# Token-major projections 512 columns wide, weights loaded unit by unit, and TensorE transposes in the first segment of a hybrid mLSTM and DeltaNet layer

## The chip, the cores and the metric

The kernel runs on one core of a Trainium2 chip. Its engines are TensorE (PE: matmuls, and PEld for its weight loads), VectorE (DVE), ScalarE (ACT), GpSimd (POOL) and SyncE (SP, which issues nearly all transfers). The metric is the device time of one execution in microseconds (us), as the median of three runs.

## What is computed

One decoder layer over 2048 tokens of width 1024 in float32. Both kinds of heads read the same normalised input; four mLSTM heads and eight gated DeltaNet (GDN) heads are worked off in chunks, gated, and projected back:

```python
h = rms_norm(x, attn_norm[l])
proj = jnp.einsum('bsd,dp->bsp', h, w_in[l])
(mq, mk, mv, mo, mz, mi, mf, gqkv, gz, gb, ga) = jnp.split(proj, split_points, axis=-1)
h_m = mlstm_chunkwise(q_m, k_m, v_m, i_pre, f_pre)
y_m = h_m * jax.nn.sigmoid(mo) * jax.nn.silu(mz)          # h_m normalised before
qkv = jax.nn.silu(causal_depthwise_conv(gqkv, g_conv[l]))
o_g = gated_delta_chunkwise(q_g, k_g, v_g, log_alpha, beta)
y_g = merge_heads(o_g) * jax.nn.silu(gz)                  # o_g normalised before
x = x + jnp.einsum('bsm,md->bsd', jnp.concatenate([y_m, y_g], -1), w_out[l])
return rms_norm(x, final_norm)
```

## The kernel before

The tokens are cut into four segments of 512. In a segment the work goes pair by pair (n = 0 to 3: two GDN heads and one mLSTM head), each pair in two windows. Window P projects the pair's GDN columns: gk, gq and gv feature-major (`proj_fm`: the weights stand still and 512 tokens move, two tiles `pf_...` of 24 matmuls for each), then gz token-major (`proj_tm`: 128 tokens stand still and 256 weight columns move, four tiles `pt_gz` of 24 matmuls). For n = 0 gz comes first. Window M projects mq and mk feature-major, and then mv, mo and mz token-major, 256 columns each, 96 matmuls each. Every product is three matmuls, since weights and input are split into a high and a low part (`hi`, `lo`; `hh`, `hl`). The last segment has its windows in another order. The output projection (`po`) follows after the last segment.

A projection's tile lies in one of three PSUM buffers (`psj`); another five (`psc`) serve everything else. A tile's buffer is free for the third tile after it when its readers are done: ACT's copy into `xin` for the GDN tiles, whose depthwise convolution (three taps, L675) and silu (L681) DVE does; for mv ACT's copy (L512) and DVE's low part `vlo` (L515; not for n = 3); for gz ACT's tanh and DVE's product `gg` (L703); for mz ACT's tanh (L525) and DVE's L526. In the first segment (`raw`) the input isn't normalised yet, and tiles are scaled as they are read: `ps * rbc0` in place by DVE for feature-major, ACT with `rs0` (L365) for token-major.

k and v of the GDN are needed token-major as well. Where the tables `KTR` and `VT` (rows: first segment, middle segments, last; columns: n) hold 1, DVE does it with 32-row stream transposes (`ktok`, `gv`, L488); where they hold 0, PE transposes 128x128 blocks (`ktp`, `vp`).

Between the projections' steps `window` puts other work into PE's order, each as a stream spread over a fraction of the window (`WIN` = 41.6 cost units): `g_prep` (ktok, the products `kk`, q's norm, and the forward substitution `tb`/`xb` that inverts 32-row blocks on DVE, L825 and L829) at the start of M; `g_level` (`dmz`, `zp`, `fp`, `zq`, `fq`) and the first `CH_N` = 6 of 14 steps of `g_chain` (`sp`, `R`, `vq`, `su`, `op`, `SS`) in the next P, the other steps in the next M; `m_chunks` of the mLSTM head (`nd`, `up`, `CN`, with k transposed by DVE into `kw`, and `ptt` made from a row `nm` that SP fetches) in the next P. At the end of the segment the next segment's input is loaded and squared (`rms_stats`).

PE's order is what the code writes (`tc.manual_schedule`). The other engines are ordered when the kernel is built, by a list scheduler with priorities, and that order is fixed: an engine whose next instruction isn't ready waits.

Weights come from DRAM in units of 512 KB, with a ring of ten of them (`wu`). In the first segment each group is loaded raw, split into high and low parts, and the parts are stored for the later segments; later `load_w` fetches a group's four units one group ahead, when `next_w` is called.

Of the kernel before, what the change touches and what calls it, by code (L numbers as in the profile page):

```python
# [65 lines left out]
def hybrid_layer(  # L66
# [80 lines left out]

    def unit(ncol, dt, nm):
        return wp.tile([P, HK, ncol], dt, tag="wu", name=nm, bufs=10)

    def load_w(key, src, ncol, nm, between=None):

        if key in parts_d:
            his, los = ([unit(ncol, F32R, f"{p_}_{nm}_{i}") for i in range(2)] for p_ in ("whi", "wlo"))
            for i in range(2):
                for part, t_ in enumerate((his[i], los[i])):
                    nc.sync.dma_start(t_.bitcast(F32), parts_d[key][part, i])
            return his, los
        return split_w(key, src, ncol, nm, between)
# [1221 lines left out]
```

## Time and profile before

| | |
|---|---|
| median of three runs | 2320.91 us (2320.58 to 2321.42) |
| profiled execution | 2320.7 us |
| its span in the trace | 2318.9 us |
| busy share of the span: PE, DVE, ACT, POOL | 95%, 81%, 38%, 35% |
| first segment | 7 to 513.3 us |
| second, third, fourth segment | 513.3 to 987.2, to 1459.8, to 1938 us |
| rest of the output projection | 1938 to 2318.9 us |

Times in the trace are counted from the span's start. A window of the second segment is named by n: P(2) runs from 756.5 to 813.8, M(2) from 813.8 to 869.6. PE is the engine that is busy nearly always; the matmul records overlap, so one that lasts 0.28 us in the records can follow the last after 0.12.

### The profile page before, as it was taken

To read this page: it belongs to the slowest core of one execution; us is meant where nothing else is said; L and a number is where in the kernel's file an instruction comes from. 1 tells how busy PE (TensorE), PEld (TensorE's weight loads), DVE (VectorE), ACT (ScalarE), POOL (GpSimd) and SP (SyncE) were. 2 spreads that over 40 slices of the span, in tenths; PEclk is the share of its full clock that TensorE was granted. 3 is DMA by queue.
4 is the path that set the end of the run, shared out by engine and by line. 5 is a ranking of instruction groups with operands and counts; after the bars stand their busy time and mean duration, and the time that the engine had idled before them with its cause. 6 is when DMAs were issued, how large, how long until landed. Compare 5 with 4: busy or idle time off the path is not lost.

```text
span 2318.9 us, 41978 instructions
## 1 busy us (share of the span) xinstructions
PE 2212.4 (95%) x14750; PEld 1964.7 (85%) x14750; DVE 1888.6 (81%) x5359; ACT 875.5 (38%) x2351; POOL 800.4 (35%) x1220
## 2 busy tenths in 40 slices
PE   8889999998999999998999999999999999999998
PEld 7778888887989898888898989888988997788887
DVE  7989898997988888879888888798757737887784
ACT  5545555544342424343334243443344234111111
POOL 4646565561211111423021214221212114555543
PEclk9999999999999999999999999999999999999999
DMA  7766667674445454654455546454546454222321
GB/s 268 248 222 225 227 216 256 212 257 159 159 160 182 160 191 159 231 182 155 154 185 175 188 166 236 146 180 172 188 163 210 160 195 151 84 94 94 102 84 64
DMA packets 183323, 409.20 MB, mean 176 GB/s; under 512 B 51736, under 2 KB 84632, under 8 KB 183112
## 3 DMA queue, kind: packets, MB, share of 16 engines
q1 hardware_dynamic: 182392, 405.74, 51.4%
q8 instruction: 116, 1.90, 0.3%
q14 instruction: 95, 0.78, 0.1%
q10 hardware_dynamic: 720, 0.79, 0.1%
HBM read 309.68 MB, written 96.90 MB: 175 GB/s over the span
## 4 chain that ended last, share of the span: by engine, by line
PE 56%; DVE 30%; DMA 7%; ACT 3%; issue 2%; POOL 1%; SPq 1%; ACTq 0%; POOLq 0%; DVEq 0%
PE po L1237 5%; PE po L1236 5%; PE po L1235 5%; DVE ktok L488 3%; DVE xb L829 3%; DVE tb L825 3%; DVE kw L488 2%; DVE gv L488 2%; PE pt_mo L359 2%; PE pt_mo L360 2%; PE pt_mo L361 2%; PE pt_gz L361 2%; PE pt_mz L359 2%; PE pt_gz L360 2%; PE pt_gz L359 2%
## 5 line engine op out<-in xcount | busy, mean ns | idle before, releaser
L1196 DVE STREAM_TRANSPOSE ytt<-yl 32x256 f32<-32x256 f32 x448 | 195.3, 436 | 45.4 <-POOL ylo L1164 39.4
L993 POOL TENSOR_TENSOR gms<-gms,nhalf 128x2 f32<-128x2 f32 x64 | 47.2, 738 | 413.6 <-DVE gms L991 408.5
L825 DVE TENSOR_TENSOR tb<-xb,lbt 128x248 f32<-128x248 f32 (+30 forms) x496 | 168.0, 339 | 21.0 <-DMA lbt<-l_d 8.0
L829 DVE TENSOR_TENSOR xb<-xb,tb 128x248 f32<-128x248 f32 (+30 forms) x496 | 168.7, 340 | 12.7
L359 PE MATMUL pt_mv<-whi_M,hh 128*128 128x256 f32 x512 | 150.5, 294 | 14.4 <-DVE vlo L515 10.5
L359 PE MATMUL pt_gz<-whi_P,hh 128*128 128x256 f32 (+1 forms) x512 | 153.1, 299 | 1.4 <-ACT whi_P L175 1.1
L359 PE MATMUL pt_mz<-whi_M,hh 128*128 128x256 f32 x512 | 149.5, 292 | 4.0 <-DVE tz L526 3.4
L359 PE MATMUL pt_mo<-whi_M,hh 128*128 128x256 f32 x512 | 149.0, 291 | 1.7 <-DVE vlo L515 1.7
L361 PE MATMUL pt_gz<-whi_P,hl 128*128 128x256 f32 (+1 forms) x512 | 148.5, 290 | 1.9 <-DVE hl L336 1.9
L360 PE MATMUL pt_gz<-wlo_P,hh 128*128 128x256 f32 (+1 forms) x512 | 148.5, 290 | 0.8 <-DVE wlo_P L178 0.8
L361 PE MATMUL pt_mv<-whi_M,hl 128*128 128x256 f32 x512 | 146.9, 287 | 0.0
L360 PE MATMUL pt_mv<-wlo_M,hh 128*128 128x256 f32 x512 | 146.8, 287 | 0.0
L360 PE MATMUL pt_mz<-wlo_M,hh 128*128 128x256 f32 x512 | 145.2, 284 | 0.0
L361 PE MATMUL pt_mz<-whi_M,hl 128*128 128x256 f32 x512 | 145.2, 284 | 0.0
L361 PE MATMUL pt_mo<-whi_M,hl 128*128 128x256 f32 x512 | 144.5, 282 | 0.0
L360 PE MATMUL pt_mo<-wlo_M,hh 128*128 128x256 f32 x512 | 144.5, 282 | 0.0
L1244 ACT ACTIVATE jkf<-xr 128x512 f32<-128x512 f32 (+1 forms) x33 | 20.4, 619 | 266.9 <-DVE xr L1242 143.5
L488 DVE STREAM_TRANSPOSE ktok<-gk 32x128 f32<-32x128 f32 x384 | 116.2, 303 | 5.4
L488 DVE STREAM_TRANSPOSE gv<-xingv 32x128 f32<-32x128 f32 x384 | 116.1, 302 | 5.4
L1235 PE MATMUL po<-woh,yh 128*128 128x512 f32 (+1 forms) x297 | 114.6, 386 | 1.1 <-ACT yh L1162 1.1
L1236 PE MATMUL po<-wol,yh 128*128 128x512 f32 (+1 forms) x297 | 114.7, 386 | 0.9 <-POOL wol L1042 0.9
L1237 PE MATMUL po<-woh,ylo 128*128 128x512 f32 (+1 forms) x297 | 114.8, 387 | 0.1
(403 smaller groups left out, 7581.0 us busy)
## 6 DMA issues: line engine op xcount, KB each, us to landing
whi_M<-wdM SPq DMA_DIRECT2D x96, 512.0 KB, 3.9
wlo_M<-wdM SPq DMA_DIRECT2D x96, 512.0 KB, 5.6
whi_P<-wdP SPq DMA_DIRECT2D x90, 512.0 KB, 4.0
wlo_P<-wdP SPq DMA_DIRECT2D x90, 512.0 KB, 5.1
wraw_M<-in_wg_dram SPq DMA_DIRECT2D x32, 512.0 KB, 6.7
wdM<-whi_M SPq DMA_DIRECT2D x32, 512.0 KB, 3.7
wdM<-wlo_M SPq DMA_DIRECT2D x32, 512.0 KB, 5.3
wraw_P<-in_wg_dram SPq DMA_DIRECT2D x30, 512.0 KB, 6.3
```

The lines of the kernel that those rows point to most:

```text
L359: nc.tensor.matmul(ps, lhsT=hh[k][:, ts], rhs=hi, start=(k == 0), stop=False)
L360: nc.tensor.matmul(ps, lhsT=hh[k][:, ts], rhs=lo, start=False, stop=False)
L361: nc.tensor.matmul(ps, lhsT=hl[k][:, ts], rhs=hi, start=False, stop=(k == KT - 1))
L488: nc.vector.transpose(dst[32 * a:32 * a + 32, :, 32 * b:32 * b + 32], s4[32 * b:32 * b + 32, :, a, :])
L825: nc.vector.tensor_tensor(tb[:, :, 0:n], xb[:, :, i:i + 1].broadcast_to([P, 8, n]), lbt[:, i:i + 1, i + 1:32].broadcast_to([P, 8, n]), op= ...
L829: nc.vector.tensor_tensor(xs, xs, tb[:, :, 0:n], op=ALU.subtract)
L993: nc.gpsimd.tensor_tensor(ms, ms, nhalf[:, 0:2], op=ALU.pow)
L1196: nc.vector.transpose(ytt[32 * b:32 * b + 32, :, 32 * a:32 * a + 32], y3[32 * a:32 * a + 32, :, 32 * b:32 * b + 32])
L1235: nc.tensor.matmul(ps, lhsT=yh, rhs=woh, start=(k == 0), stop=False)
L1236: nc.tensor.matmul(ps, lhsT=yh, rhs=wol, start=False, stop=False)
L1237: nc.tensor.matmul(ps, lhsT=ylo, rhs=woh, start=False, stop=(k == 15))
L1244: nc.scalar.activation(jk[:, 0:n], xr[:, cs], AF.Square, accum_out=ssf[:, i:i + 1])
```

## The change

- From the second segment on, mo and mz of a head are one projection 512 columns wide (`proj_tm_wide`): two tiles at a time, step by step in turn, in two passes over the weights. gz of pair n and mv of head n are likewise one (`wide_z`: n = 1 to 3 of the second and third segment, n = 1 of the fourth), and it stands at the start of M, ahead of mq and mk. Its tiles are called `pt_mv`; gz is the left half, mv the right.
- Window P then ends with gv. The cost units by which streams are spread are 31 for such P windows and 52 for such M windows, and the chain gets 4 of its steps in P instead of 6 (`CH_NW`; n = 1 to 3 of the middle segments).
- The stored parts of two groups that go together lie side by side, and units are loaded whenever the ring has one free (`freed`, `pump`).
- In the first segment k and v are transposed by PE in all pairs, DVE writes the scaled feature-major tiles straight to their place (`fm_out`), and mv and mo are scaled by the instruction that reads them.

```diff
+NU = 10
...
+CH_NW = 4
...
-VT = ((0, 1, 1, 1), (1, 1, 1, 1), (1, 0, 0, 0))
-KTR = ((0, 1, 1, 1), (1, 1, 1, 1), (0, 1, 0, 0))
+VT = ((0, 0, 0, 0), (1, 1, 1, 1), (1, 0, 0, 0))
+KTR = ((0, 0, 0, 0), (1, 1, 1, 1), (0, 1, 0, 0))
...
+    ring = {"free": NU}
+    coming = []
...
+        if isinstance(key, list):
+            w = Weights(nm, 512, 2)
+            kept = parts_d[key[0]][0]
+            w.due = [((p_, i), kept[p_, i // 2, :, i % 2 * 2:i % 2 * 2 + 2]) for i in range(4) for p_ in range(2)]
...
+    def pump():
+        while coming and ring["free"] > 0:
+            w = coming[0]
+            at, src = w.due.pop(0)
+            t_ = w.units[at] = unit_(w.rows, w.n, F32R, f"w{at[0]}_{w.nm}_{at[1]}")
+            nc.sync.dma_start(t_.bitcast(F32), src)
+            ring["free"] -= 1
+            if not w.due:
+                wready.append(coming.pop(0))
+
+    def freed(n):
+        ring["free"] += n
+        if not wloads:
+            pump()
...
-        kept = parts_d[key] = ypool.tile([2, 2, P, HK, ncol], F32, tag=f"wd{nm}", name=f"wd{nm}")
+        pair = next((p_ for p_ in WIDE if key in p_), None)
+        c0 = pair.index(key) * ncol if pair else 0
+        if c0:
+            kept = parts_d[pair[0]][0]
+        else:
+            kept = ypool.tile([2, 2, P, HK, 512 if pair else ncol], F32, tag=f"wd{nm}", name=f"wd{nm}")
+        parts_d[key] = kept, c0, ncol
...
+    WIDE = [[("M", n, 2), ("M", n, 3)] for n in range(4)] + [[("P", n, 3), ("M", n, 1)] for n in range(1, 4)]
+
+    def wide_z(seg, n):
+
+        return seg > 0 and n > 0 and not (seg == NSEG - 1 and n > 1)
...
+                if seg:
+                    if kind == "M" and i > 1:
+                        if i == 2:
+                            wgets.append((WIDE[n], nm))
+                    elif kind == "M" and i == 0 and wide_z(seg, n):
+                        wgets += [(WIDE[3 + n], f"V{seg}_{n}"), (key, nm)]
+                    elif (kind, i) not in (("M", 1), ("P", 3)) or not wide_z(seg, n):
+                        wgets.append((key, nm))
...
     def prefetch_w(between=None):
         if wloads:
-            wready.append(load_w(*wloads.pop(0), between))
+            wready.append(split_w(*wloads.pop(0), between))
+            if not wloads:
+
+                coming.extend(get_w(*g_) for g_ in wgets)
+                ring["free"] = NU - 8
...
+            if c0 and k % HK == HK - 1:
+                freed(2)
             if k == KT - 1:
-                if raw[0]:
-                    nc.vector.tensor_tensor(ps, ps, rbc0, op=ALU.mult)
                 done(ps)
             yield 0.65
 
...
+    def fm_out(dst, ps, scale=None):
+
+        if not raw[0]:
+            if scale is None:
+                nc.scalar.copy(dst, ps)
+            else:
+                nc.scalar.activation(dst, ps, AF.Copy, scale=scale)
+        elif scale is None:
+            nc.vector.tensor_tensor(dst, ps, rbc0, op=ALU.mult)
+        else:
+            nc.vector.scalar_tensor_tensor(dst, ps, scale, rbc0, op0=ALU.mult, op1=ALU.mult)
+
+    def tm_done(ps, t, done, scaled=True):
+        if raw[0] and scaled:
             nc.scalar.activation(ps, ps, AF.Copy, scale=rs0[:, t:t + 1])
         done(ps, t)
...
+    def proj_tm_wide(w, nm, done):
+
+
+        for t0 in range(0, NCH, 2):
+            pss = [psj.tile([P, T], F32, tag="pj", name=f"pt_{nm}_{t0 + i}") for i in range(2)]
+            for k in range(KT):
+                for i in range(2):
+                    tm_step(pss[i], w, t0 + i, k)
+                    if t0 and i and k % 2:
+                        freed(2)
+                    if k == KT - 1:
+                        done(pss[i], t0 + i)
+                    yield 0.65
...
         def keep_v(ps, t):
-            nc.scalar.copy(vt[:, t, 0:256], ps)
+            if raw[0]:
+                nc.scalar.activation(vt[:, t, 0:256], ps, AF.Copy, scale=rs0[:, t:t + 1])
+            else:
+                nc.scalar.copy(vt[:, t, 0:256], ps)
             if fast:
+                v_ = vt[:, t, 0:256].bitcast(F32)
                 with tc.high_priority(VPR):
-                    nc.vector.tensor_tensor(vlo[:, t, :], ps, vt[:, t, 0:256].bitcast(F32),
-                                            op=ALU.subtract)
...
+        def gates(ps, t):
+            nc.scalar.activation(G[:, t, :], ps[:, 0:256], AF.Tanh, scale=0.5)
+            gate(ps[:, 256:512], t)
+
+        if wide_z(seg, n):
+            z_gate = g_gate(seg, n, rp, None)
+
+            def both(ps, t):
+                z_gate(ps, t)
+                keep_v(ps[:, 256:512], t)
+            yield from proj_tm_wide(next_w(), f"mv{s_}", both)
+        w = next_w()
+        yield from proj_fm(w, 0, f"mq{s_}",
+                           lambda ps: fm_out(qT, ps, DK ** -0.5))
+        yield from proj_fm(w, P, f"mk{s_}", lambda ps: fm_out(kT, ps))
+        if not wide_z(seg, n):
+            yield from proj_tm(next_w(), f"mv{s_}", keep_v, False)
+        w = next_w()
+        if seg:
+            yield from proj_tm_wide(w, f"mo{s_}", gates)
+            return
+        yield from proj_tm(w, f"mo{s_}", lambda ps, t: nc.scalar.activation(
+            G[:, t, :], ps, AF.Tanh, scale=rs0h[:, t:t + 1] if raw[0] else 0.5), False)
+        w = next_w()
+
         yield from proj_tm(w, f"mz{s_}", gate)
...
-        if pr:
+        if pr and not wide_z(seg, pr):
             yield from g_proj_z(seg, pr, r, st)
...
-                    nc.scalar.copy(xi[:, 3:T + 3], ps)
+                    fm_out(xi[:, 3:T + 3], ps)
                     nc.gpsimd.tensor_copy(halo[:, fi, :], xi[:, T:T + 3])
-                    nc.scalar.activation(d, ps, AF.Copy, scale=conv_c[:, fi, 3:4])
+                    nc.scalar.activation(d, xi[:, 3:T + 3] if raw[0] else ps, AF.Copy,
+                                         scale=conv_c[:, fi, 3:4])
...
+    WIN, WINP, WINM = 41.6, 31.0, 52.0
...
+    def ch_n(seg, n):
+
+        return CH_NW if n and seg and seg < NSEG - 1 else CH_N
+
+    def win(kind, seg, n):
+        return WIN if not wide_z(seg, n) else WINP if kind == "P" else WINM
...
-                    streams += [(lvl[q], NLV, LV0, LV1, PRI), (chain[q], CH_N, CH0, 1.01, PRI)]
+                    streams += [(lvl[q], NLV, LV0, LV1, PRI), (chain[q], ch_n(seg, n), CH0, 1.01, PRI)]
...
                     if (n - 1) % 4 in chain:
-                        streams.append((chain[(n - 1) % 4], NCS - CH_N, 0.02, CH1, PRI))
+                        streams.append((chain[(n - 1) % 4], NCS - ch_n(seg, n), 0.02, CH1, PRI))
```

What moves is shown for one pair, n = 2 of the second segment (names end in `1_2` and a tile's numbers). PE around the end of P, before: the last steps of the mLSTM stream, and then gz, for which P goes on with 96 matmuls.

```order
4128 L598 MATMUL nd1_1_3_9633<-cn1_1_3_tb_9634,qws1_1_9195 128x258
4129 L596 MATMUL up1_1_3_9644<-mv1_1_8403,kws1_1_pt_9274 128x258
4130 L597 MATMUL up1_1_3_9644<-vlo1_1_8687,kws1_1_pt_9274 128x256
4131 L598 MATMUL up1_1_3_9644<-mv1_1_8403,kws1_1_nm_9275 128x258
4132 L359 MATMUL pt_gz1_2_0_9673<-whi_P1_2_3_0_9438,hh_155 128x256
4133 L360 MATMUL pt_gz1_2_0_9673<-wlo_P1_2_3_0_9440,hh_155 128x256
4134 L361 MATMUL pt_gz1_2_0_9673<-whi_P1_2_3_0_9438,hl_156 128x256
4135 L359 MATMUL pt_gz1_2_0_9673<-whi_P1_2_3_0_9438,hh_155 128x256
```

Now gv is followed at once by the wide tiles, and this is where they change from the first pass to the second: kk's last product, the first pass's last steps, and the first matmuls of the third and the fourth tile.

```order
3947 L921 MATMUL kk1_2_1_1_9340<-kh1_2_1_9276,kl1_2_1_nm_9278 128x256
3948 L425 MATMUL pt_mv1_2_0_9188<-w0_V1_2_3_9135,hh_155 128x512
3949 L426 MATMUL pt_mv1_2_0_9188<-w1_V1_2_3_9137,hh_155 128x512
3950 L427 MATMUL pt_mv1_2_0_9188<-w0_V1_2_3_9135,hl_156 128x512
3951 L425 MATMUL pt_mv1_2_1_9189<-w0_V1_2_3_9135,hh_155 128x512
3952 L426 MATMUL pt_mv1_2_1_9189<-w1_V1_2_3_9137,hh_155 128x512
3953 L427 MATMUL pt_mv1_2_1_9189<-w0_V1_2_3_9135,hl_156 128x512
3954 L425 MATMUL pt_mv1_2_2_9450<-w0_V1_2_0_8773,hh_155 128x512
3955 L426 MATMUL pt_mv1_2_2_9450<-w1_V1_2_0_8775,hh_155 128x512
3956 L427 MATMUL pt_mv1_2_2_9450<-w0_V1_2_0_8773,hl_156 128x512
3957 L425 MATMUL pt_mv1_2_3_9451<-w0_V1_2_0_8773,hh_155 128x512
```

Six matmuls lie between the last of tile `pt_mv1_2_0` and the first of `pt_mv1_2_3`, which takes its buffer; before, two whole tiles of 24 lay between them.

DVE up to the first vlo of the same pair, before: the last of kk's products into ua, q's norm, ptt, the transposes kw of mk, a step of the chain, vlo.

```order
1404 L807 SCALAR_TENSOR_TENSOR ua1_2_9839<-kk1_2_1_1_9970,scol1_2_9883,ua1_2_9839 128x256 x2
1405 L862 COPY ssq1_2_9857<-qs1_2_10063 32x2x4 x4
1406 L995 SCALAR_TENSOR_TENSOR gyt1_1_1_9962<-op1_1_1_9954,gms1_1_1_9961,gg1_1_8255 128x128 x2
1407 L865 TENSOR_SCALAR cq41_2_10093<-ssq1_2_9857 128x8
1408 L541 SCALAR_TENSOR_TENSOR ptt1_2_10591<-nm1_2_10589,ccol1_6922,negmask_198 128x128 x4
1409 L488 STREAM_TRANSPOSE kw1_2_10674<-mk1_2_9819 32x4x32 x16
1410 L953 SCALAR_TENSOR_TENSOR R1_1_2_10127<-sp1_1_2_10128,neg1_6936,vr1_1_2_9834 128x128 x2
1411 L515 TENSOR_TENSOR vlo1_2_10104<-pt_mv1_2_0_10105,mv1_2_9820 128x256
1412 L515 TENSOR_TENSOR vlo1_2_10104<-pt_mv1_2_1_10138,mv1_2_9820 128x256
```

And now:

```order
1362 L966 TENSOR_REDUCE qs1_2_9443<-qtp1_2_1_9458 128x16
1363 L584 STREAM_TRANSPOSE gv1_2_1_9121<-xingv1_2_1_9155 32x4x32 x4
1364 L930 SCALAR_TENSOR_TENSOR ua1_2_9218<-kk1_2_1_1_9340,scol1_2_9262,ua1_2_9218 128x256 x2
1365 L826 SCALAR_TENSOR_TENSOR gg1_2_9187<-gtz1_2_0_9352,pt_mv1_2_0_9188 128x256
1366 L826 SCALAR_TENSOR_TENSOR gg1_2_9187<-gtz1_2_1_9360,pt_mv1_2_1_9189 128x256
1367 L660 SCALAR_TENSOR_TENSOR ptt1_2_9891<-nm1_2_9889,ccol1_6729,negmask_199 128x128 x3
1368 L983 TENSOR_TENSOR qs1_2_9443<-qs1_2_9443 32x32
1369 L660 SCALAR_TENSOR_TENSOR ptt1_2_9891<-nm1_2_9889,ccol1_6729,negmask_199 128x128
1370 L616 TENSOR_TENSOR vlo1_2_9186<-pt_mv1_2_0_9188,mv1_2_9183 128x256
1371 L616 TENSOR_TENSOR vlo1_2_9186<-pt_mv1_2_1_9189,mv1_2_9183 128x256
```

The transposes kw and the end of q's norm (copies to ssq, cq4) come behind vlo now, the first two gg have come in ahead of it, and the transposes of gv stand right before.

## Rows read from the trace of the kernel before

**Rows 1.** The page, part 1: busy time of each engine.
```profile
PE 2212.4 (95%) x14750; PEld 1964.7 (85%) x14750; DVE 1888.6 (81%) x5359; ACT 875.5 (38%) x2351; POOL 800.4 (35%) x1220
```

**Rows 2.** Stretches: length, busy PE, PEld, DVE, ACT, POOL; clock, DMA share, GB/s.
```profile
129.70:513.30 383.60, 351.57 (x2446) 317.45 (x2446) 343.97 (x931) 196.19 (x509) 217.69 (x317) 0.96 0.66 227
513.30:987.20 473.90, 455.38 (x3273) 411.87 (x3272) 401.55 (x1235) 178.06 (x502) 108.97 (x185) 0.99 0.52 177
1459.80:1938.00 478.20, 471.72 (x3488) 427.66 (x3487) 333.28 (x1055) 178.13 (x527) 94.26 (x163) 1.00 0.51 172
```

**Rows 3.** The same columns within P(2) and M(2); the sum is 763.40 to 840.10.
```profile
756.50:799.70 43.20, 42.78 (x287) 35.14 (x286) 37.60 (x106) 19.67 (x47) 5.85 (x16) 1.00 0.49 162
799.70:813.80 14.10, 14.10 (x122) 14.10 (x121) 13.79 (x43) 6.91 (x22) 4.38 (x7) 1.00 0.43 138
...
sum 76.70, PE 75.34 PEld 66.73 DVE 68.37 ACT 30.79 POOL 18.43; mean PE 37.67 PEld 33.36 DVE 34.19 ACT 15.40 POOL 9.22
```

**Rows 4.** Timeline of the pair, DVE (one SP): start, length, what, idle before.
```profile
763.40 1.54 DVE L675 SCALAR_TENSOR_TENSOR gk<-xingk,conv_c,gk 128x512 f32<-128x512 f32 x2 [1.46 <-ACT gk L673]
...
826.26 0.32 SPq L537 DMA_DIRECT2D nm<-rows  x1
...
831.27 1.14 DVE L541 SCALAR_TENSOR_TENSOR ptt<-nm,ccol,negmask 128x128 f32<-128x128 f32 x4 [2.04 <-DMA nm<-rows]
...
839.70 0.41 DVE L515 TENSOR_TENSOR vlo<-pt_mv,mv 128x256 fp32r<-128x256 f32 x1
```

**Rows 5.** Timeline of the pair, PE: P's start and the fourth mv tile's.
```profile
756.47 0.39 PE L347 MATMUL pf_gk<-hh,whi_P 128*128 128x512 f32 x1
...
837.76 0.28 PE L359 MATMUL pt_mv<-whi_M,hh 128*128 128x256 f32 x1
...
838.36 0.28 PE L361 MATMUL pt_mv<-whi_M,hl 128*128 128x256 f32 x1
839.59 0.75 PE L959 MATMUL vq<-R,E 128*128 128x128 f32 x4 [0.94 <-DVE R L953]
840.17 0.39 PE L359 MATMUL pt_mv<-whi_M,hh 128*128 128x256 f32 x1
```

**Rows 6.** Output projection's matmuls alone in a stretch: length, busy PE, PEld, DVE; clock.
```profile
2000.00:2030.00 30.00, 30.00 (x132) 24.46 (x131) 1.36 (x2) 1.00 0.34 118
```

**Rows 7.** DVE by line, 831.3 to 840.2: count, busy us, mean ns, idle before.
```profile
L488 DVE STREAM_TRANSPOSE kw<-mk 32x128 f32<-32x128 f32 x16 | 4.8, 303 | 1.9 <-ACT mk L503 1.7
```

**Rows 8.** Work on mz's tiles alone: length, busy PE, PEld, DVE, ACT.
```profile
1331.00:1337.00 6.00, 5.80 (x50) 5.62 (x49) 0.84 (x2) 0.77 (x2) 1.00 0.49 188
```

**Rows 9.** Stretches at and behind waits of PE, columns as in rows 2.
```profile
149.00:152.20 3.20, 0.03 (x1) 0.03 (x1) 3.11 (x8) 3.15 (x9) 3.09 (x4) 1.00 0.91 271
152.20:155.60 3.40, 3.26 (x37) 2.69 (x38) 3.26 (x11) 1.06 (x3) 0.50 (x3) 0.56 0.97 382
...
502.10:507.00 4.90, 4.90 (x22) 4.82 (x23) 4.69 (x14) 4.25 (x12) 3.60 (x7) 0.50 0.00 0
...
526.40:531.00 4.60, 4.56 (x29) 4.25 (x29) 3.49 (x19) 0.86 (x3) 0.77 (x3) 1.00 0.17 57
```

**Rows 10.** DVE by line, 129.7 to 513.3: count, busy us, mean ns.
```profile
L488 DVE STREAM_TRANSPOSE ktok<-gk 32x128 f32<-32x128 f32 x96 | 29.0, 303 | 1.4
L488 DVE STREAM_TRANSPOSE gv<-xingv 32x128 f32<-32x128 f32 x96 | 29.0, 302 | 1.2
```

**Rows 11.** Timeline, PE: two transposes of v in the last segment.
```profile
1833.03 0.39 PE L929 MATMUL vp<-ident,gv 128*128 128x128 f32 x2
1833.25 0.61 PE L950 MATMUL sp<-SS,gk 128*128 128x128 f32 x4
```

**Rows 12.** What PE waited for, 129.7 to 513.3: us in total, times, longest.
```profile
PE sp L950 <- DVE SS L981: 7.4, 3, 2.6
PE fp L894 <- ACT dmz L889: 6.7, 3, 3.5
```

**Rows 13.** The page, part 6: weight units, KB each, us from issue to landing.
```profile
wlo_M<-wdM SPq DMA_DIRECT2D x96, 512.0 KB, 5.6
```

More of the change, by code (lines that the diff above doesn't have):

```diff
@@ L146, in hybrid_layer, with unit_, __init__, part @@
     parts_d = {}
+    def unit_(rows, ncol, dt, nm):
+        return wp.tile([P, rows, ncol], dt, tag="wu", name=nm, bufs=NU)
     def unit(ncol, dt, nm):
[L149 to L154, printed above, removed]
-            for i in range(2):
[L156 to L159, printed above, removed]
+        return unit_(HK, ncol, dt, nm)
+    class Weights:
+        def __init__(self, nm, ncol, rows):
+            self.nm, self.n, self.rows, self.units, self.due = nm, ncol, rows, {}, []
+        def part(self, p_, k):
+            return self.units[p_, k // self.rows][:, k % self.rows, :]
+    ring = {"free": NU}
+    coming = []
+    def get_w(key, nm):
+        if isinstance(key, list):
[3 more added lines that the diff above has]
+        else:
+            kept, c0, n = parts_d[key]
+            w = Weights(nm, n, HK)
+            for i in range(2):
+                for p_ in range(2):
+                    w.due.append(((p_, i), kept[p_, i, :, :, c0:c0 + n]))
+        return w
+    def pump():
[11 more added lines that the diff above has]
+            pump()
     def split_w(key, src, ncol, nm, between):
@@ L229, in hybrid_layer @@
     rs0 = cst.tile([P, NCH], F32, name="rs0")
+    rs0h = cst.tile([P, NCH], F32, name="rs0h")
     rbc0 = cst.tile([P, T], F32, name="rbc0")
@@ L356, in tm_step @@
     def tm_step(ps, w, t, k):
-        hi, lo = (p_[k // HK][:, k % HK, :] for p_ in w)
+        hi, lo = (w.part(p_, k) for p_ in range(2))
         ts = slice(t * P, (t + 1) * P)
@@ L500, in m_proj @@
         r.update(q=qT, k=kT, v=vt, g=G)
-        yield from proj_fm(w, 0, f"mq{s_}",
-                           lambda ps: nc.scalar.activation(qT, ps, AF.Copy, scale=DK ** -0.5))
-        yield from proj_fm(w, P, f"mk{s_}", lambda ps: nc.scalar.copy(kT, ps))
-        w = next_w()
         if fast:
@@ L691, in g_proj_z, with g_gate @@
     def g_proj_z(seg, pr, r, st):
+        gate = g_gate(seg, pr, r, st)
+        yield from (proj_tm_first if seg == 0 and pr == 0 else proj_tm)(next_w(), f"gz{seg}_{pr}", gate)
+    def g_gate(seg, pr, r, st):
         s_ = f"{seg}_{pr}"
-        w = next_w()
         G = wkp.tile([P, NCH, 256], F32, tag="gg", name=f"gg{s_}", bufs=2)
@@ L709, in gate @@
                     beta[:, t, :], ps[:, 272:280], -1.0, 85.0, op0=ALU.mult, op1=ALU.min)
-        yield from (proj_tm_first if seg == 0 and pr == 0 else proj_tm)(w, f"gz{s_}", gate)
+        return gate
     def g_prep(seg, pr, r, st):
@@ L1147, in hybrid_layer @@
                     keep = (mch[n],)
-                window(m_proj(seg, n, r), WIN, streams, keep)
+                window(m_proj(seg, n, r, prs[n]), win(kind, seg, n), streams, keep)
     hstack.close()
```

53 lines of the change are left out of this document (29 added, 24 removed).

## Prediction, made before the changed kernel ran

> **What bounds the kernel now.** I read the page's busy line first [rows 1]: PE is busy for 95% of the span, so in most stretches PE's own work sets the end. The table of stretches [rows 2] shows where it doesn't. In the last three pairs of the first segment (129.7 to 513.3) PE is busy 351.6 of 383.6 us at a mean clock of 0.96, while DVE has 344.0 us of work. In the second segment PE is busy 455.4 of 473.9 us and DVE 401.6. So DVE is never far behind, and the question is in which order its work falls due. That is read in one steady pair (second segment, n = 2, P window from 756.47, M window from 813.8) [rows 3]: while PE runs the six feature-major projections, 43.2 us, DVE is busy for 37.6; while PE runs gz, 14.1 us, DVE is busy for 13.8. DVE works off in gz's time what the projections left: it starts the first convolution at 763.40 and gets to vlo of mv's first tile at 839.70 [rows 4], 76.7 us later, with 68.4 us of work in them [rows 3]. PE needs that vlo for the first matmul of mv's fourth tile (three PSUM buffers, so the fourth tile takes the first one's), and starts it at 840.17 [rows 5], 0.06 us after vlo ends. Here DVE already arrives last, with nothing to spare, although gz, mq, mk and two more mv tiles lie in between to give it time.
>
> **Part 1: wider matmuls.** 19 projections (12 mo+mz, 7 gz+mv) turn 3648 matmuls of 256 columns into 1824 of 512. The narrow ones start 0.120 us apart (837.76 to 838.36 in five steps) [rows 5]; 132 wide ones share 30.0 us, 0.230 each with the overlap of their ends [rows 6]. Two narrow less one wide is 0.010 us, by the closer spacing of 0.119 some 0.008: 1824 of them give 15 to 18, I take **-17** (-12 to -20). The Trainium skill ("TensorE: Matmul & The Clock Gate", Back-to-back issue gap) gives an isolated matmul N/2.4 + 2.5 ns, so a merged pair would save only the 2.5 ns; by it this term is an estimated -5, and the sum below 12 us higher. The rows are of this kernel's own shapes, and the measured spacing decides.
>
> **Part 2: gz moves behind P, and shares its tiles with mv.** For n = 1 to 3 of the two middle segments and n = 1 of the last, P now ends with gv, and M begins with the wide gz+mv, two tiles at a time in two passes, out of the same three buffers. The fourth tile takes the first one's buffer, and between the last matmul of the one and the first of the other stand only six, 1.4 us. The buffer is free when ACT has copied mv and DVE has done gg and vlo of the first tile.
> PE's side: up to the end of gv PE's order is as before, 43.2 us [rows 3]; then 51 wide matmuls (11.7), 24 of kk at 0.12 (2.9) and 8 of 128 columns at about 0.1 (0.8). PE would be there 58.6 us after P's start.
> DVE's side: from the first convolution to vlo of the first tile DVE has 174 instructions where it had 206. Gone are 16 transposes kw at 0.303, 4.85 us [rows 7], two of the four gg (0.8), and smaller ones of the chain and of q's norm (some 3.4): 9.0 us. Of the 76.7 us, 2.04 were a wait for the transfer nm [rows 4] and 1.9 a wait for mk [rows 7]; neither comes last any more, since kw is gone and nm, which is asked for behind the last kk, is there 5.0 us later (826.26 to 831.27) [rows 4], near 63, while DVE gets to ptt near 68. So 76.7 - 9.0 - 3.9 = 63.8 us after the convolution, which starts 6.9 after P: vlo is done at 70.7, and PE **waits 12.1 us**. If none of DVE's waits goes, it is 16.0; if all its idle time closes up, 68.4 - 9.0 = 59.4, it is 7.7. I take 12, the row-by-row value, for n = 1 and 2 of both middle segments; n = 1 has 1.5 us more of DVE's work ahead of vlo, which is within the bounds. For n = 3 mv has no vlo and gg is the release, 2.4 us earlier: 9.5 (5 to 13.5); ACT's copy stands behind the squares of the next segment's x there and comes at about the same time. In the last segment DVE has less to do (333.3 us of 478.2) [rows 2]: 3 (0 to 5). Together 4 x 12 + 2 x 9.5 + 3 = **+70** (41 to 96).
> The Trainium skill ("Perfetto Trace Analysis", Matmuls) says both that larger matmuls are more efficient and that independent groups should rotate through PSUM banks so that one's evacuation overlaps the next one's matmuls. By the first half alone this part would add no wait, and the sum would come to -17 + 5 - 27 = -39; by the second it adds one, as two tiles at a time out of three buffers leave 1.4 us for an evacuation. The row at 840.17 bears out the second, since even the older rotation was used up to its last 0.1 us.
> Who else is held up: behind PE's wait stand mq, mk and the next steps of the chain, all of PE's, so it isn't made up. DVE then idles near M's end, where the next P can't start early.
> Some of PE's present waits vanish in this, such as the 0.94 us for R just ahead of that matmul [rows 5]: **-5** (0 to -10).
>
> **Part 3: mo+mz wide.** The last tile waits for the first one's two tanh (0.385 each) and one DVE step (0.42) [rows 8]: about 1.2 to 1.6 us with their handing over, against 1.4 us of cover (two steps of 0.69). 12 x 0.4 = **+5** (0 to 12).
>
> **Part 4: the clock.** After waits of 3 to 4 us PE is at the lower level for a while: mean 0.56 in 152.2 to 155.6, behind 3.2 us without work, and 0.50 in 502.1 to 507.0, but 1.00 in 526.4 to 531.0, behind another [rows 9]. So a long wait costs 0 to 2.5 us more. Six waits of 9 us and over: **+10** (0 to 18).
>
> **Part 5: first segment.** 192 stream transposes leave DVE in the three pairs, 29.0 + 29.0 us [rows 10]; PE gets 48 transposes, some 0.11 each by a pair that starts at 1833.03 with the next work at 1833.25 [rows 11], +5. PE's idle time there is 32.0 us (383.6 less 351.6); the two largest waits are 7.4 us for DVE's SS and 6.7 for ACT behind dmz [rows 12], and the others are for DVE's results too. With 17% of DVE's work gone I let 26 of the 32 go, and 6 of the clock: a mean of 0.96 over 383.6 us means some 30 us at the half level, in which half a matmul's pace is lost: up to 15 us, of which I take 6. -26 - 6 + 5 = **-27**. The bounds are -12 (waits halved, no clock) and -36 (all of both). The products that DVE writes straight out replace ones that it did in place, at the same count; ACT's saved copies are off the path.
>
> **Part 6: loads as units come free.** A unit lands 5.6 us after its issue or sooner [rows 13] and the ring has ten, so a projection's next unit is there before PE asks: 0. If the cover were gone, a late unit would cost that time once per window.
>
> **The sum.** -17 + 70 - 5 + 5 + 10 - 27 = +36. The profiled execution took 2320.7 (span 2318.9), 0.2 below the median of 2320.91: 2320.7 + 36 = 2356.7, rounded to **2356**.
>
> **The rivals.** (a) DVE closes up, and the change is faster. All idle time goes from its queue, vlo is ready at 66.3 or sooner, the waits come to 41 or less, the clock stays up, the first segment gives 36: -20 + 36 - 8 + 2 + 2 - 36 = -24, 2297. It decides where vlo stands: if it is done by some 65 us after P's start (all waits about 34 us), the whole is even. For it speaks DVE's 8.3 us of idle time in the 76.7; against it, that some of these are hand-overs within DVE's own chains, which stay. 24%. (b) The two effects cancel, within 0.2% (4.6 us, about what a measurement of this kernel can tell from no change): 2321, 7%. (c) The wait takes its upper end, since DVE's waits stay and the denser P window adds others for dmz and R: 96 - 12 - 2 + 10 + 18 - 12 = +98, 2419; more likely halfway, 2385. 14%. Forecast 55%.
>
> **The numbers.** Faster 0.25 (a and its edge), same 0.07, slower 0.68. The range goes from (a)'s side, 2300, to (c)'s nearer half, 2388, and leaves out about a tenth at either end.
>
> **What would show it.** Right: in the windows with gz+mv one wait of PE of 8 to 16 us ahead of the fourth pt_mv tile, released by DVE's vlo (n = 1, 2) or gg or ACT's copy (n = 3), DVE busy without a gap up to it and idle late in M; pairs of 113 us becoming 123; the first segment 20 us and more shorter, PE's idle there under 10; wide matmuls 0.230 apart. Wrong: no such wait, or one under 5 us (then DVE's queue is shorter than I make it); the first segment unchanged (then POOL or the weights' splitting bind it, not DVE); waits for weight units; or the lower clock level without a wait ahead of it.

## The result, and the profile after

The changed kernel takes **2413.2 us** (2410.0 to 2424.6, four runs) against 2321.2 before: 1.0405 of it, 95% interval 1.037 to 1.044. It was forecast at 2356, in a range up to 2388: the direction was right, and the loss is two and a half times as large. The profiled execution is the slowest of the four (2424.6; span 2422.8), so its stretches add up to some 10 us more than the median.

The page's busy line, which answers [rows 1]: PE works 28 us more than before (a matmul at half clock counts as busy for longer), and its share falls from 95% to 92%.

```profile
PE 2240.3 (92%) x12974; PEld 1901.9 (78%) x12974; DVE 1860.9 (77%) x5168; ACT 857.0 (35%) x2293; POOL 802.5 (33%) x1220
```

Stretches (length; busy PE, PEld, DVE, ACT, POOL; clock; DMA share; GB/s), from the first gk matmul of a pair to that of the next: n = 1, 2 and 3 of the second segment, then the third segment.

```profile
626.00:763.00 137.00, 118.08 (x629) 97.51 (x628) 101.77 (x313) 42.27 (x121) 20.95 (x37) 0.91 0.44 146
763.00:892.00 129.00, 115.37 (x631) 96.04 (x630) 99.71 (x305) 42.16 (x120) 20.42 (x37) 0.93 0.46 153
892.00:1048.00 156.00, 136.79 (x762) 115.20 (x761) 119.89 (x362) 53.93 (x150) 47.56 (x79) 0.92 0.49 164
1048.00:1569.00 521.00, 466.82 (x2607) 389.33 (x2607) 413.16 (x1249) 180.66 (x502) 110.29 (x184) 0.94 0.49 160
```

The pair of n = 2 took 113.0 us before, and 128.9 now. Where PE waited, in the whole execution (what for, us in total, times, longest):

```profile
PE pt_mv L425 <- DVE vlo L616: 39.3, 6, 9.9
PE pt_mo L425 <- DVE tz L620: 26.0, 8, 8.6
PE zq L1028 <- DVE dmz L1023: 25.8, 9, 5.5
PE pt_mv L425 <- ACT mv L608: 16.9, 3, 8.0
PE vq L1082 <- DVE R L1076: 15.7, 8, 3.6
```

The first and the fourth line are the predicted wait for mv's fourth tile (but for 1.0 us, which lie in n = 0); the second and the third are waits of a size that the prediction didn't have. The first of them in n = 2 of the second segment, PE's and DVE's timeline, to be read against [rows 4, 5] (P starts at 763.2):

```profile
770.23 0.75 DVE L795 SCALAR_TENSOR_TENSOR gk<-xingk,conv_c,gk 128x512 f32<-128x512 f32 x1 [2.60 <-ACT gk L792]
...
827.28 3.44 DVE L584 STREAM_TRANSPOSE gv<-xingv 32x128 f32<-32x128 f32 x11
...
836.58 0.87 DVE L660 SCALAR_TENSOR_TENSOR ptt<-nm,ccol,negmask 128x128 f32<-128x128 f32 x3
...
837.97 0.75 DVE L616 TENSOR_TENSOR vlo<-pt_mv,mv 128x256 fp32r<-128x256 f32 x2
...
828.78 0.39 PE L427 MATMUL pt_mv<-w_V,hl 128*128 128x512 f32 x1
838.53 0.76 PE L425 MATMUL pt_mv<-w_V,hh 128*128 128x512 f32 x1 [9.36 <-DVE vlo L616]
```

No idle time stands ahead of ptt any more: nm was asked for at 830.05 and, at the 5.0 us that it took before [rows 4], was there by about 835, while DVE comes to ptt at 836.58. Its vlo of the first tile, the first of the two in the record at 837.97, lets PE go on 9.36 us after the third tile's first matmuls.

How long each pair took, in us, from the traces (from its first gk matmul to the next pair's; "rest" runs to the end), with the kernels of the experiments:

| kernel | first segment, from P(0)'s gk | n = 0 | n = 1 | n = 2 | n = 3 | n = 0 | n = 1 | n = 2 | n = 3 | rest |
|---|---|---|---|---|---|---|---|---|---|---|
| before | 508.8 | 105.2 | 117.5 | 113.0 | 137.1 | 106.5 | 116.1 | 112.9 | 136.7 | 840.1 |
| after | 493.7 | 107.4 | 137.2 | 128.9 | 155.9 | 108.5 | 129.9 | 126.7 | 156.2 | 853.4 |
| no wide projections | 490.4 | 103.0 | 113.4 | 112.9 | 135.8 | 106.5 | 113.5 | 113.2 | 138.4 | 842.0 |
| mo+mz wide only | 490.4 | 106.1 | 111.9 | 113.0 | 142.1 | 107.1 | 112.3 | 115.7 | 148.4 | 842.5 |
| gz moved, nothing wide | 490.7 | 103.0 | 121.0 | 119.6 | 144.5 | 106.6 | 119.3 | 118.7 | 143.9 | 844.9 |
| after, PE transposes | 492.6 | 100.3 | 116.5 | 113.5 | 146.6 | 99.4 | 114.2 | 113.6 | 147.0 | 855.1 |

### The profile page after: what moved, and what is told of

The parts are those of the page before. It is cut to its first block, busy times and chain, and to the rows that moved or that the text cites. A ratio compares the mean times of both kernels' runs of the same rounds, so it can differ in the third digit from the quotient of the medians.

```text
span 2422.8 us, 38195 instructions
## 1 busy us (share of the span) xinstructions
PE 2240.3 (92%) x12974; PEld 1901.9 (78%) x12974; DVE 1860.9 (77%) x5168; ACT 857.0 (35%) x2293; POOL 802.5 (33%) x1220
## 4 chain that ended last, share of the span: by engine, by line
PE 45%; DVE 36%; DMA 7%; issue 4%; POOL 3%; ACT 3%; SPq 1%; POOLq 0%; ACTq 0%; DVEq 0%
PE po L1368 5%; PE po L1366 5%; PE po L1367 4%; DVE xb L952 4%; DVE tb L948 4%; DVE gv L584 4%; DVE ktok L584 3%; PE pt_mo L425 3%; PE pt_mo L427 2%; PE pt_mo L426 2%; DVE kw L584 2%; DVE ua L930 1%; DVE gv L795 1%; PE pf_gk L413 1%; PE pf_gk L415 1%
## 5 line engine op out<-in xcount | busy, mean ns | idle before, releaser
L1327 DVE STREAM_TRANSPOSE ytt<-yl 32x256 f32<-32x256 f32 x448 | 195.3, 436 | 45.4 <-POOL ylo L1295 39.3
L425 PE MATMUL pt_mo<-w_M,hh 128*128 128x512 f32 x384 | 162.8, 424 | 31.6 <-DVE tz L620 26.0
L427 PE MATMUL pt_mo<-w_M,hl 128*128 128x512 f32 x384 | 155.8, 406 | 0.0
L426 PE MATMUL pt_mo<-w_M,hh 128*128 128x512 f32 x384 | 155.8, 406 | 0.0
L425 PE MATMUL pt_mv<-w_V,hh 128*128 128x512 f32 x224 | 96.4, 430 | 55.2 <-DVE vlo L616 38.3
L425 PEld LDWEIGHTS pt_mo<-w_M,hh 128*128 128x128 f32 x384 | 75.5, 197 | 51.9 <-DVE tz L620 30.4
L215 POOL TENSOR_TENSOR wlo_M<-wraw_M,whi_M 128x256 fp32r<-128x256 f32 x128 | 97.1, 792 | 49.6 <-ACT whi_M L212 49.6
L1330 POOL TENSOR_TENSOR ytt<-ytt,gain_c 128x256 f32<-128x256 f32 x120 | 82.8, 720 | 70.0 <-DVE ytt L1327 69.8
L215 POOL TENSOR_TENSOR wlo_P<-wraw_P,whi_P 128x256 fp32r<-128x256 f32 x104 | 88.2, 874 | 52.1 <-ACT whi_P L212 52.1
L425 PEld LDWEIGHTS pt_mv<-w_V,hh 128*128 128x128 f32 x224 | 45.3, 202 | 65.8 <-issue 39.9
L795 DVE SCALAR_TENSOR_TENSOR gk<-xingk,conv_c,gk 128x512 f32<-128x512 f32 x96 | 74.3, 774 | 26.0 <-ACT gk L792 24.1
L426 PE MATMUL pt_mv<-w_V,hh 128*128 128x512 f32 x224 | 92.5, 413 | 0.0
L427 PE MATMUL pt_mv<-w_V,hl 128*128 128x512 f32 x224 | 92.3, 412 | 0.0
```

The source lines that it names most:

```text
L215: eng.tensor_tensor(lo[:, ks, :], raw_[:, ks, :], hi[:, ks, :].bitcast(F32), op=ALU.subtract)
L425: nc.tensor.matmul(ps, lhsT=hh[k][:, ts], rhs=hi, start=(k == 0), stop=False)
L426: nc.tensor.matmul(ps, lhsT=hh[k][:, ts], rhs=lo, start=False, stop=False)
L427: nc.tensor.matmul(ps, lhsT=hl[k][:, ts], rhs=hi, start=False, stop=(k == KT - 1))
L795: nc.vector.scalar_tensor_tensor(d, xi[:, tap:tap + T], conv_c[:, fi, tap:tap + 1], d, op0=ALU.mult, op1=ALU.add)
L1327: nc.vector.transpose(ytt[32 * b:32 * b + 32, :, 32 * a:32 * a + 32], y3[32 * a:32 * a + 32, :, 32 * b:32 * b + 32])
```

## The experiments

All times are medians of four to ten runs; before is 2320.7 to 2321.7 beside them.

**1. The first segment's transposes alone.** In the kernel before:

```diff
-VT = ((0, 1, 1, 1), (1, 1, 1, 1), (1, 0, 0, 0))
-KTR = ((0, 1, 1, 1), (1, 1, 1, 1), (0, 1, 0, 0))
+VT = ((0, 0, 0, 0), (1, 1, 1, 1), (1, 0, 0, 0))
+KTR = ((0, 0, 0, 0), (1, 1, 1, 1), (0, 1, 0, 0))
```

> The kernel before, with one thing of the change: in the first segment PE transposes k and v instead of DVE. Theory (DVE is what the first segment waits for): the changed kernel's first two windows and three pairs took 512.0 us against 526.7, and this alone gives all of it, 2306 us (2303 to 2311). Rival (the gain comes from DVE writing the scaled tiles straight out, which saves ACT a copy): 2317 or more, and the rest of the gain shows in the kernel without wide projections.

Measured: **2307.7**, 0.9943 of before (0.9929 to 0.9958): 13 us. The theory's figure holds. What it said of the rest doesn't: the next kernel gains more.

**2. Nothing wide.** The changed kernel with `wide_z` false, mo and mz narrow and `CH_NW = 6`:

```diff
-        return seg > 0 and n > 0 and not (seg == NSEG - 1 and n > 1)
+        return False
...
-        if seg:
-            yield from proj_tm_wide(w, f"mo{s_}", gates)
-            return
...
```

> The changed kernel with every token-major projection 256 wide again, in its old place, so what is left is the first segment's change and the loading of units as they come free. Theory (all of the loss hangs on the wide projections): 2306 us (2302 to 2312). Rival (the unit-wise loads or the order of SP's queue cost something): 2325 or more, with PE waiting for weight units.

Measured: **2293.1**, 0.9880 (0.9852 to 0.9908). So the first segment's change and the loads unit by unit bring 27.6 us, twice what the transposes bring alone; in the table 18 of it lie in the first segment (where the transposes alone bring 11) and 8 in the middle ones. What brings the rest, DVE's writing straight out, the scaling of mv and mo, or the loads, wasn't separated. The whole loss hangs on the wide projections together with what came with them (gz's place, the window costs, the chain's steps): 2413.2 - 2293.1 = 120 us.

**3. mo+mz wide, gz and mv as before.** The first edit of experiment 2 alone, with `CH_NW = 6`.

> The changed kernel with mo+mz wide and gz and mv as they were (gz at the end of P, 256 wide). Theory (gz's time at the end of P is what DVE needs): the waits ahead of mv's fourth tile (57 us) and for dmz (26) go, mo+mz alone saves 1152 x 0.009 = 10 us and keeps some of its own waits: 2310 (2300 to 2325). Rival (two wide tiles at a time out of three buffers cost wherever they stand, and the clock with them): 2350 or more.

Measured: **2309.7**, 0.9953 (0.9935 to 0.9971). Taken off in this order, 103 of the 120 us belong to gz+mv and 17 to mo+mz. In the table mo+mz loses in n = 3 (142.1 and 148.4 against 135.8 and 138.4) and gains nothing worth naming elsewhere.

**4. DVE relieved.** The changed kernel, and in the middle segments PE transposes k and v:

```diff
-VT = ((0, 0, 0, 0), (1, 1, 1, 1), (1, 0, 0, 0))
-KTR = ((0, 0, 0, 0), (1, 1, 1, 1), (0, 1, 0, 0))
+VT = ((0, 0, 0, 0), (0, 0, 0, 0), (1, 0, 0, 0))
+KTR = ((0, 0, 0, 0), (0, 0, 0, 0), (0, 1, 0, 0))
```

> The changed kernel, and PE transposes k and v in the middle segments too, which takes 19 us per pair from DVE's queue ahead of mv's first tiles and gives PE 16 transposes. Theory (DVE comes late to the release): the waits ahead of mv's fourth tile in the middle segments go (57 us to under 15), those for dmz too, the clock gets half of its loss back: 2330 (2315 to 2350). Rival (the buffer is too tight whatever DVE has to do): 2390 or more.

Measured: **2322.7**, 1.0006 (0.9992 to 1.0019). Taking 19 us of transposes per pair off DVE gives back 90 us, of which the table shows 16 in n = 0, where nothing of gz+mv is wide. PE's waits in it:

```profile
PE pt_mo L425 <- DVE tz L620: 24.7, 8, 9.0
...
PE pt_mv L425 <- ACT mv L608: 6.4, 3, 2.7
PE zq L1028 <- DVE dmz L1023: 5.2, 3, 2.8
...
PE pt_mv L425 <- DVE vlo L616: 3.6, 4, 0.9
```

The waits for vlo fall from 39.3 to 3.6, those for dmz from 25.8 to 5.2: both came from the work that stood ahead of them on DVE. Those for tz stay.

**5. Four buffers for the projections, four for the rest.** The first segment's small statistics tile goes to the projections' buffers as well, since five tiles are wanted at once there:

```diff
-    psj = ctx.enter_context(tc.tile_pool(name="psj", bufs=3, space=PSUM))
-    psc = ctx.enter_context(tc.tile_pool(name="psc", bufs=5, space=PSUM))
+    psj = ctx.enter_context(tc.tile_pool(name="psj", bufs=4, space=PSUM))
+    psc = ctx.enter_context(tc.tile_pool(name="psc", bufs=4, space=PSUM))
```

> The changed kernel with four PSUM buffers for the projections and four for everything else, instead of three and five. Theory (PE waits because a buffer has to come back from a late DVE): mv's fourth tile has a buffer of its own, the release is wanted 11 us later, by mq, and of the 57 us ahead of the fourth tile 45 go, with half of the clock's loss; the other stages lose a few us for want of a fifth buffer: 2350 (2330 to 2375). Rival (DVE is behind for the whole pair, and the wait only moves on): 2395 or more.

Measured: **2352.0**, 1.0137 (1.0121 to 1.0153). A buffer more takes away 61 us without relieving DVE of anything. What stays is another group of waits (PE's, the largest three):

```profile
PE zq L1028 <- DVE dmz L1023: 26.2, 8, 4.0
PE vq L1082 <- DVE R L1076: 21.8, 7, 6.7
PE lbp L539 <- DVE cq L535: 11.3, 4, 5.1
```

**6. One wide tile at a time.** The wide projection with the loops of the narrow one:

```diff
-        for t0 in range(0, NCH, 2):
-            pss = [psj.tile([P, T], F32, tag="pj", name=f"pt_{nm}_{t0 + i}") for i in range(2)]
+        for t in range(NCH):
+            ps = psj.tile([P, T], F32, tag="pj", name=f"pt_{nm}_{t}")
             for k in range(KT):
-                for i in range(2):
...
```

> The changed kernel with the wide projections one tile at a time instead of two in turn; everything else, gz's place too, is as changed. Between a tile's end and the reuse of its buffer then lie two tiles of 5.5 us, and the fourth gz+mv tile comes 4.8 us later. Theory (buffer cover and DVE's lateness together make the wait): the waits ahead of mv's fourth tile fall from 9 to 4 us, those for tz go: 2413 - 29 - 20 - 10 = 2355 (2335 to 2385). Rival (a group's eight units must all stay until its last tile, so the next group's come late): 2400 or more, with PE waiting for units.

Measured: **2353.9**, 1.0141 (1.0123 to 1.0159). It gives back 59 us, about as much as the fourth buffer. The waits ahead of the fourth tile and for tz are all but gone, and the rival's price shows too:

```profile
PE zq L1027 <- DVE dmz L1022: 23.0, 9, 3.5
PE vq L1081 <- DVE R L1075: 19.4, 17, 3.3
PE pf_mq L413 <- DMA w_M<-wdM: 13.5, 6, 2.9
...
PE pf_mq L415 <- DMA w_M<-wdM: 5.8, 6, 2.0
PE pt_gz L425 <- DMA w_P<-wdP: 5.7, 2, 4.1
...
PE pt_gz L426 <- DMA w_P<-wdP: 2.8, 2, 1.9
```

The last four are 27.8 us of waiting for weight units, which the changed kernel doesn't have. The total came out as forecast although more of the buffers' waits went than the theory said, since these came in their place.

**7. gz moved, and nothing wide.** In the kernel of experiment 2, with the change's window costs (31 and 52) and `CH_NW = 4`:

```diff
-        if pr and not wide_z(seg, pr):
+        if pr and not moved(seg, pr):
             yield from g_proj_z(seg, pr, r, st)
...
+        if moved(seg, n):
+            yield from g_proj_z(seg, n, rp, None)
         w = next_w()
         yield from proj_fm(w, 0, f"mq{s_}",
```

> The kernel without wide projections, with one thing more: gz of the same pairs as in the change stands at the start of M instead of the end of P, still 256 columns wide, one tile at a time, with the change's window costs and chain steps; mq, mk, mv, mo and mz follow as ever. Theory (gz at the end of P is the time in which DVE catches up, whatever the width): of the 103 us between the changed kernel and the one with gz and mv as they were, 60 went with more buffer cover and some 40 did not; so this costs about that: 2293 + 35 = 2328 (2312 to 2345), with waits of PE for dmz and R and for gg. Rival (only the two wide tiles in turn cost): 2293 to 2302.

Measured: **2338.0**, 1.0069 (1.0048 to 1.0089): 45 us for gz's place, together with the window costs and the chain's steps that go with it, and with no matmul wider. PE's waits in it:

```profile
PE zq L1027 <- DVE dmz L1022: 21.8, 7, 3.7
...
PE pf_mk L413 <- DVE gg L825: 10.5, 6, 2.6
```

The waits for dmz are among those that the fourth buffer and the single tile left over. So gz+mv's 103 us are some 45 for gz's place with its settings and, by the difference, some 58 for the width and the two tiles in turn out of three buffers. That experiments 5 and 6 give back about as much fits, but isn't a second measurement of it: both relieve mo+mz too, and each has a price of its own. gz moved with the streams spaced as before wasn't run, so the place and the settings aren't separated.

**8. PE kept busy in the wait.** Thirty matmuls of 512 columns ahead of the fourth gz+mv tile, whose result nobody reads:

```diff
+NFILL = 30
...
+                    if t0 and i and k == 0 and nm[:2] == "mv":
+                        fill = psc.tile([P, T], F32, tag="cp", name=f"fill{nm}")
+                        for _ in range(NFILL):
+                            nc.tensor.matmul(fill, lhsT=hh[0][:, 0:P], rhs=hh[0], start=True, stop=True)
                     tm_step(pss[i], w, t0 + i, k)
```

> The changed kernel with 30 matmuls of 512 columns, whose result nobody reads, ahead of mv's fourth wide tile, that is inside PE's wait of 8 to 10 us (30 x 0.23 = 6.9 us). Theory (PE's clock falls because it stands idle, and costs more behind the wait): the waits shrink to 1 to 3 us, the stretches at half clock behind them go, and the time falls by 15 us (8 to 25): 2398. Rival (the clock's loss has nothing to do with these waits): 2413 or more, with as much time at half clock.

Measured: **2415.7** (2410.8 to 2417.5), 1.0414 (1.0394 to 1.0434): no gain. The waits for vlo did shrink:

```profile
PE pt_mv L426 <- DVE vlo L621: 10.9, 6, 2.9
```

and the mean clock is 0.971 to 0.973 in its four runs, where the changed kernel's have 0.959 to 0.967. In the profiled executions the time at half clock falls from 201 to 130 us, but about half of this lay in PE's idle time, where it costs nothing: outside it the fall is from 145 to 107. The middle segments go from 1050.8 to 1039.2; but these two executions are the changed kernel's slowest and this kernel's fastest, and over the runs nothing is left. One of the seven waits, in the last segment, was only 1.2 us long, so there the spare matmuls held PE up themselves: that pair took 122.0 us, against 119.7. So the theory isn't borne out, and where the rest of the better clock's time went stays open.

**9. PE's transposes, with mo and mz narrow for n = 3.** On top of experiment 4 (the lists of weight groups go along):

```diff
...
-        if seg:
+        if seg and n < 3:
             yield from proj_tm_wide(w, f"mo{s_}", gates)
             return
```

> The changed kernel with PE transposing k and v in the middle segments too, and for n = 3 mo and mz as two projections 256 wide. Theory (in n = 3 DVE stands at dmz, waiting for E's transfer, with tz behind it in its order, and the narrow tiles have more cover): the two waits of 9 us for tz go, with the clock behind them: 2322.7 - 22 = 2300 (2294 to 2308). Rival (another wait takes their place): 2316 or more.

Measured: **2304.2**, 0.9936 (0.9911 to 0.9961): 18.5 us less where 22 were expected, within the theory's range. The waits for tz fall from 24.7:

```profile
PE pt_mo L425 <- DVE tz L620: 5.4, 8, 1.5
```

The rival has a part too: PE's waits for R rise from 13.6 to 20.8 us.

**10. PE's transposes, nothing wide.** Experiment 2 with the tables of experiment 4.

> The kernel without wide projections, with PE transposing k and v in the middle segments too. It differs from the kernel with PE's transposes (2322.7) and from the one with mo and mz narrow for n = 3 (2304.2) by the wide projections alone, with DVE relieved in all. Theory (a merged pair saves 0.008 us, 19 projections 15 us, and that is lost again in waits for the release): about 2293 + 128 transposes x 0.11 - 10 for n = 0 = 2297 (2288 to 2306). Rival (once DVE is relieved, wide pays): 2310 or more.

Measured: **2295.1**, 0.9887 (0.9864 to 0.9911). Even with DVE relieved and n = 3 mended, the kernel with wide projections (2304.2) doesn't beat the one without; it differs from it by gz's place and the settings as well as by the width.

**11. PE's transposes for n = 0 only, nothing wide.** The middle rows are (0, 1, 1, 1).

> The kernel without wide projections, with PE transposing k and v for n = 0 of the middle segments alone, where DVE has the build of the segment's input besides. In the kernel with PE's transposes these two windows pairs took 100.3 and 99.4 us against 103.0 and 106.5 here. Theory (DVE is what n = 0 waits for): 2293 - 8 = 2285 (2280 to 2291), the fastest so far. Rival (that gain came from mo+mz being wide): 2292 or more.

Measured: **2285.1**, 0.9841 (0.9818 to 0.9864), faster than both kernels by 36 and 128 us. n = 0 of the two middle segments takes 100.3 and 98.1 us instead of 103.0 and 106.5.

## Why the prediction was right or wrong

**Wide matmuls, -17: right in kind.** In the trace after, 512 columns start 0.231 us apart (median) and the narrow ones left 0.119 to 0.120, so a merged pair saves 0.008: 15 us. This is worked out from the spacing; no run shows it by itself, since PE waits in the same windows.

**The wait for mv's fourth tile, +70: mechanism right, size near.** Forecast 12 us each for n = 1 and 2, 9.5 for n = 3, 3 in the last segment; found 9.95, 9.36, 9.61 and 9.39, then 7.7 and 8.0, then 1.2, together 55. vlo came 68.1 us after the first convolution (770.23 to 838.4), later than the 63.8 worked out: DVE had 61.5 us of work in it, not 59.4, and in place of the two waits that went as forecast (nm and mk) stand others, for ACT's xingk (1.8), PE's up (1.5) and ACT's gq (1.0). But PE was later too: it stood at the fourth tile 66 us after P's start and not at 58.6. The step "up to the end of gv PE's order is as before, 43.2 us" was wrong: gv ended 49.4 us after P's start, because PE had waited for dmz and run at half clock in P. That the wait came out near the forecast is in part luck, since both sides were late. In n = 3 ACT's copy comes last, behind the squares of the next input, as the prediction had it (ACT's and PE's timeline, n = 3 of the second segment):

```profile
964.29 1.06 ACT L131 ACTIVATE xt<-xt 128x1024 f32<-128x1024 f32 x1 [1.23 <-DMA xt<-in_x_dram]
965.26 0.19 ACT L131 ACTIVATION_READ_ACCUMULATOR xt<-xt 128x1 f32 x1
965.58 0.37 ACT L608 COPY mv<-pt_mv 128x256 f32<-128x256 f32 x1
...
966.00 0.80 PE L425 MATMUL pt_mv<-w_V,hh 128*128 128x512 f32 x1 [7.69 <-ACT mv L608]
```

**"Some of PE's present waits vanish", -5: wrong.** Waits for R vanished, and as many for dmz came in. PE's waits over the two middle segments, before:

```profile
PE vq L959 <- DVE R L953: 10.8, 10, 2.0
PE zq L905 <- DVE dmz L900: 5.8, 6, 2.1
```

and after:

```profile
PE zq L1028 <- DVE dmz L1023: 19.7, 6, 5.5
...
PE vq L1082 <- DVE R L1076: 1.1, 1, 1.1
```

All waits there but those ahead of the token-major tiles pt_mv, pt_mo and pt_mz sum to 29 us before and to 29 after. The step looked only at what PE waits for near the fourth tile. In P of n = 2, DVE's and PE's timeline, before (P starts at 756.47):

```profile
767.87 4.72 DVE L488 STREAM_TRANSPOSE ktok<-gk 32x128 f32<-32x128 f32 x15
...
776.45 0.43 DVE L900 STREAM_TRANSPOSE dmz<-E 32x256 f32<-32x256 f32 x1
776.94 1.14 PE L905 MATMUL zq<-dmz,ua 64*64 64x64 f32 x16 [0.41 <-DVE dmz L900]
```

and after (P starts at 763.25):

```profile
777.85 2.85 DVE L584 STREAM_TRANSPOSE ktok<-gk 32x128 f32<-32x128 f32 x9
780.73 0.75 DVE L795 SCALAR_TENSOR_TENSOR gk<-xingk,conv_c,gk 128x512 f32<-128x512 f32 x1
781.51 0.43 DVE L1023 STREAM_TRANSPOSE dmz<-E 32x256 f32<-32x256 f32 x1
...
782.00 0.58 PE L1028 MATMUL zq<-dmz,ua 64*64 64x64 f32 x3 [2.85 <-DVE dmz L1023]
```

dmz's transpose stands behind k's in DVE's order in both, and DVE comes to it no later now: 18.3 us after P's start, and 20.0 before. What changed is PE. P's streams are pressed into 31 cost units instead of 41.6, so PE asks for dmz 15.9 us after P's start, and not 20.1. The kernel of experiment 7 spaces its streams in the same way, and its waits for dmz are much the same (21.8 us against 25.8, in the whole execution; before, 6.4 behind the first segment). The rival (c), "the denser P window adds others for dmz and R", had dmz right and R wrong. Its 2419 was the nearest figure, but by luck: it rests on a wait of 96 us for the fourth tile, which was 55, and on 18 for the clock, which was some 40; it had 14%.

**mo+mz, +5: undersized.** It was worked from the durations of two tanh and a product against the cover; the waits for tz are 26.0 us, of which two of 8.6 and 8.2 in n = 3, and another 5.6 lie ahead of the wide tiles of n = 0, for mv's vlo. DVE's order was not read there. It stands at dmz, whose E isn't there yet, with tz behind it (DVE's and PE's timeline, n = 3):

```profile
1013.22 0.43 DVE L1002 STREAM_TRANSPOSE dmz<-E 32x256 f32<-32x256 f32 x1 [4.20 <-DMA E<-e_d]
...
1015.85 0.41 DVE L620 SCALAR_TENSOR_TENSOR tz<-tz,pt_mo 128x256 f32<-128x256 f32 x1
...
1016.32 0.79 PE L425 MATMUL pt_mo<-w_M,hh 128*128 128x512 f32 x1 [8.60 <-DVE tz L620]
```

Experiment 3 prices the term at +17 with the saved matmul time in it, and experiment 9 removes these two waits.

**The clock, +10: undersized, in the profiled execution.** Time at half clock outside PE's idle time is 145 us against 71, which is 37 us of matmul time; the first segment got 6 us better in this, so what the change added elsewhere is 43. (Of the four runs this one has the lowest mean clock, 0.959 against 0.965 to 0.967.) Behind the six long waits that the step counted stand some 29 us at half clock, 15 of matmul time, within its bounds; it had nothing for the clock behind the waits for dmz and tz. The second row answers [rows 9]; the first stands behind the 9.36 us (columns as in the stretches above):

```profile
838.50:843.10 4.60, 4.57 (x12) 3.73 (x13) 1.40 (x8) 0.50 (x1) 0.00 (x0) 0.51 0.38 118
...
782.00:788.40 6.40, 6.40 (x31) 5.53 (x31) 3.05 (x7) 2.06 (x5) 0.19 (x1) 0.50 0.00 0
```

Whether that time could be won back by keeping PE busy is what experiment 8 didn't show.

**The first segment, -27: near by luck.** With the loads it is -27.6 (experiment 2), but only 18 of that in the first segment. In the changed kernel that segment is 15 us shorter. The step let 26 of PE's 32 us of idle time go; from the second pair's first gk matmul to the second segment's it went from 35.1 to 24.0. The transposes alone are -13 (experiment 1), and the prediction gave the direct writing and the loads nothing. Its bounds don't follow from its own figures either: waits halved and no clock is -16 + 5 = -11, and all of both -32 - 15 + 5 = -42. Part 6, 0, holds, as no wait for a weight unit stands in PE's list; the 5.6 us of [rows 13] are a median, though, and not a bound.

**The sum.** By the runs: -27.6 for the first segment and the loads, +16.6 for mo+mz (the prediction's share: -11 + 5 = -6), +103.5 for gz+mv (the prediction's share: -6 + 70 - 5 + 10 = 69), of which 45 for gz's place with its settings, come to +92. By the profiled execution, 104 us longer: PE idle for 76 us more, 37 for the clock, an estimated 5 for PE's transposes in the first segment, less 15 for the wider matmuls, together 103. So the terms that failed are the clock (+10; 43 outside the first segment), mo+mz's waits (+5; 28 more than the same tiles had before) and "some of PE's present waits vanish" (-5; none in sum), while the large term, +70, was rather too big. The step behind all three is that each wait was sized at one place, from the durations there, with the rest of PE's order taken to be as before. PE's order in P had become denser and DVE's order was fixed, so PE waited for two more things of DVE's (dmz and tz), mostly with some time at half clock behind.

## What to carry to other kernels

A projection whose evacuation is light isn't only work: at the end of a window it can be the time in which another engine catches up, and moving it moves that time, and makes the first engine ask for everything sooner. When an engine's order is fixed, ask of every result that PE wants from it what stands ahead in that order, and what that in turn waits for; a duration alone prices none of it. Before saving a few ns per matmul by wider tiles, count how long a tile's buffer is covered after the change, against what the cover was used for before.
